# A diffusion-transformer layer on one core: stores issued later in the program, and modulation sums transposed in single banks

## The chip, the cores and the metric

The kernel runs on one core of a Trainium2 chip. The metric is device time in microseconds (us), the median of the runs made. TensorE (PE) multiplies matrices into PSUM, VectorE (DVE), ScalarE (ACT) and GpSimd (POOL) work element by element, and SyncE (SP) issues the DMAs, in the order of its queue. PSUM has eight banks of 128 x 512 fp32 values.

## The reference

One layer of a hybrid diffusion backbone: 1024 latent tokens and 256 context tokens of width 1024. What matters here is the combined input projection, the merge by gates and the modulation:

```python
m_lat = (jax.nn.silu(c) @ w_mod[l] + b_mod[l]).reshape(B_, 1, N_MOD, D)
h_lat = rms_norm(x, norm_mix[l]) * (1.0 + m_lat[:, :, 1]) + m_lat[:, :, 0]
aq, ak, av, bq, bk, bv, cq, cf, cb, ci, cg, gates = features(h_lat, w_in[l], ...)
...
yc = hgrn2_bidir(cq, cf, cb, ci, cg, lbf[l], lbb[l], gn_c[l], s_f, s_b)[0]
ya = window_attn(aq, ak, av, cak, cav, sink_a[l])
yb = global_attn(bq, bk, bv, cbk, cbv)
x_mix = x + m_lat[:, :, 2] * merge_branches(ya, yb, yc, gates, w_branch[l], w_out[l])
h = rms_norm(x_mix, norm_ffn[l]) * (1.0 + m_lat[:, :, 4]) + m_lat[:, :, 3]
x = x_mix + m_lat[:, :, 5] * conv_ffn(h, w_up[l], w_dw[l], b_dw[l], w_down[l])
```

The first two parts of the modulation (`m_lat[0]`, `m_lat[1]`) are needed at the start; the other four, 1024 values each, only from the merge on.

## The kernel before

The layer runs as one program: the first modulation and the norms (to some 60 us), the context's projections, four heads of the recurrence (to some 430 us), the queries, keys and values of the two attentions (`tok_major`, 452 to 680 us), the two attentions (to some 1200 us), merge, output projection, FFN.

**Three matmuls for one.** A weight comes by one DMA as `wr` (L172), ACT casts it to a rounded high part `wh` (L175), DVE makes the low part `wl` (L176). A product is `wh*hh + wh*hl + wl*hh` (L199 to L201 with channels as rows, L209 to L211 with tokens as rows), where `hh` and `hl` are the parts of the normed input. `wr`, `wh` and `wl` have three buffers each.

**The gate unit** (`gate_unit`). Twenty-four of them make the sigmoid gates' inputs. One unit has a weight tile of 128 output channels and two halves of 512 tokens. A half is 24 matmuls into one bank `gz`; then ACT copies it to `gs` (L523, two buffers) and SP stores it to `gate_d` (L524). Outside the attentions both halves lie in one two-bank tile of tag `mm`, and the second half begins when ACT has copied the first. A unit is named by branch and number: `gz27` is branch 2, unit 7, `gs270` and `gs271` its halves.

**The token-major tiles** (`tok_major`, once for each attention `br`). For `u` in 2, 0, 1 (keys and values, then two halves of the queries) eight tiles of 128 tokens: 24 matmuls of 256 columns into `tm`, in a bank of tag `a` for even tiles and `b` for odd ones, two buffers each, taken in turn. `tm117` is attention 1, `u` 1, tile 7. In attention 1, `head_rms` squares on ACT (`hsq`, L1042), sums (L1045) and scales (L1046) on DVE, raises to the power -0.5 on POOL (`hrs`, L1047), and DVE multiplies into `qn` (L610), which is the last read of the bank for queries. Keys have one more, ACT's copy of the values into `qo` (L615). `rope` then makes `t` (L591, two rows) and `qo` (L594, L595), and SP stores `qo` (L616, L618). A gate unit follows each eight tiles.

**The other four parts of the modulation** (`mod_rest`). For each part `j`, eight loads `wmr` (L537, two buffers) are added up on DVE into `macc` (L539, L541); then eight transposes (L546) into an `mm` tile and one reduction along the free axis (L547) give the 1024 values, and `b_mod` is added (L548). `weave` puts one step of it between every few steps of `tok_major`.

**What sets the order.** The code's order decides which buffer a tile gets. The order on each engine is set by the framework's scheduler, which draws an instruction ahead when, by its own estimate, its operands are ready earlier; loads of weights have a raised priority. Each engine then runs its list strictly in that order.

Of the kernel before, what the change touches and what calls it, by code (L numbers as in the profile page):

```python
# [9 lines left out]
F32 = mybir.dt.float32  # L10
# [4 lines left out]
AX = mybir.AxisListType  # L15
# [3 lines left out]
P = 128  # L19
D = 1024  # L20
KT = D // P
# [70 lines left out]
def build(tc, ins, out, dbg=None):  # L92
    nc = tc.nc
    V, A, G, T, SP = nc.vector, nc.scalar, nc.gpsimd, nc.tensor, nc.sync
    with ExitStack() as top:
# [21 lines left out]
        def mm2(name):  # L117
            return ps.tile([P, 2, 512], F32, tag="mm", name=name)
# [160 lines left out]
        with ExitStack() as s0:  # L279
# [214 lines left out]
            for h in range(CH):  # L494
# [6 lines left out]
                for d in range(2):  # L501
# [2 lines left out]
                        T.matmul(u, kt[:, d, c], cV[:, c, h], start=c == 0, stop=c == 1)  # L504
                    A.copy(st_ctx[:, h, d], u)

        def gate_unit(pool, n, i, mode):

            w = w_unit(ins["w_cm"][U_C["gate"] + n * 8 + i], KT, P)
            for hf in range(2):  # L510
                if mode == "b":
                    z = bank("b", f"gz{n}{i}{hf}", (P, 512))
                else:
                    if hf == 0:
                        z2 = mm2(f"gz{n}{i}")
                    z = z2[:, hf]
                for k in range(KT):
                    gemm_cm(z, (w[0][:, k:k + 1], w[1][:, k:k + 1]), H, slice(hf * 512, hf * 512 + 512),
                            k0=k, first=k == 0, last=k == KT - 1)
                    if k < KT - 1:  # L520
                        yield
                gs = pool.tile([P, 512], F32, tag="gs", name=f"gs{n}{i}{hf}", bufs=2)
                A.copy(gs, z)  # L523
                SP.dma_start(gate_d[n, i][:, hf * 512:hf * 512 + 512], gs)  # L524
                yield

        def gate_units(pool, units, mode):
# [3 lines left out]
        def mod_rest(pool):  # L531

            for j in range(4):
                acc = pool.tile([P, D], F32, tag="macc", name=f"macc{j}", bufs=1)
                for k in range(KT):
                    wm = pool.tile([P, D], F32, tag="wmr", name=f"wmr{j}{k}", bufs=2)
                    SP.dma_start(wm, ins["w_mod"][k * P:(k + 1) * P, (j + 2) * D:(j + 3) * D])  # L537
                    if k == 0:
                        V.tensor_scalar(out=acc, in0=wm, scalar1=scc[:, k, 0:1], scalar2=None, op0=ALU.mult)  # L539
                    else:  # L540
                        V.scalar_tensor_tensor(out=acc, in0=wm, scalar=scc[:, k, 0:1], in1=acc,  # L541
                                               op0=ALU.mult, op1=ALU.add)
                    yield
                pm2 = mm2(f"pm2{j}").rearrange("p a (b c) -> p (a b) c", c=P)
                for i in range(KT):
                    T.transpose(pm2[:, i], acc[:, i * P:(i + 1) * P], ident)  # L546
                V.reduce_sum(out=mods[:, j], in_=pm2, axis=AX.X)  # L547
                V.tensor_tensor(out=mods[:, j], in0=mods[:, j], in1=bmod[:, (j + 2) * 8:(j + 3) * 8], op=ALU.add)  # L548
            V.scalar_tensor_tensor(out=af, in0=mods[:, 2], scalar=1.0, in1=gains[:, 1], op0=ALU.add, op1=ALU.mult)
            yield  # L550
# [5 lines left out]
        with ExitStack() as sc:  # L556
            c1 = Aligned(sc.enter_context(tc.tile_pool(name="c1", bufs=1, side="right", reuse_waits="tile")))
            masks = c1.tile([P, NMASK, HB], U32, tag="masks", name="masks")
            SP.dma_start(masks, ins["hmask"])
            late = []  # L560
            for h in range(CH):
                late = hgrn_head(nc, c1, h, proj, early, mm2, bank, ident, masks, lb, oml, st_ctx, gnc, mhalf, y_d, late)
            for n, i in gates[:4]:
                for j, _ in enumerate(gate_unit(c1, n, i, "mm")):
                    if late and j % 8 == 7:
                        late.pop(0)()

        stx.close()


        with ExitStack() as sp3:
            p3 = Aligned(sp3.enter_context(tc.tile_pool(name="p3", bufs=2, side="right", reuse_waits="tile")))
            cs = p3.tile([P, LT, 2, 32], F32, tag="cs", name="cs", bufs=1)
            SP.dma_start(cs, ins["rope"])

            tabs = {}
            for nm, g in (("A", None), ("q", qnb), ("k", knb)):
                tb = p3.tile([P, LT, 2, 2, 32], F32, tag=f"tb{nm}", name=f"tb{nm}", bufs=1)
                for r in range(2):
                    if g is None:  # L580
                        G.tensor_copy(tb[:, :, :, r], cs)
                    else:
                        G.tensor_tensor(out=tb[:, :, :, r], in0=cs,
                                        in1=g[:, None, None, r * 32:(r + 1) * 32].to_broadcast([P, LT, 2, 32]),
                                        op=ALU.mult)
                tabs[nm] = tb

            def rope(src, nh, tt, tab, dst, nm):
                t12 = p3.tile([P, 2, nh, 64], F32, tag="t12", name=f"t12{nm}")
                for w in range(2):  # L590
                    V.tensor_tensor(out=t12[:, w], in0=src,  # L591
                                    in1=tab[:, tt, w].rearrange("p r c -> p (r c)")[:, None, :].to_broadcast([P, nh, 64]),
                                    op=ALU.mult)
                V.tensor_tensor(out=dst[:, :, 0:32], in0=t12[:, 0, :, 0:32], in1=t12[:, 1, :, 32:64], op=ALU.subtract)  # L594
                V.tensor_tensor(out=dst[:, :, 32:64], in0=t12[:, 0, :, 32:64], in1=t12[:, 1, :, 0:32], op=ALU.add)  # L595

            def tok_major(br):
                for u in (2, 0, 1):
                    ws = [w_unit(ins["w_tm"][(br * 3 + u) * 2 + kh], 4, 256) for kh in range(2)]
                    for tt in range(LT):  # L600
                        nm = f"{br}{u}{tt}"
                        z = bank("ab"[tt % 2], f"tm{nm}", (P, 256))
                        gemm_tm(z, ws, H, slice(tt * P, (tt + 1) * P))
                        nh = 4 if u < 2 else 2
                        o = p3.tile([P, 256], F32, tag="qo", name=f"qo{nm}", bufs=3)
                        src = z[:, :nh * 64].rearrange("p (h e) -> p h e", h=nh)
                        if br == 1:
                            rs = head_rms(nc, p3, z[:, :nh * 64], nh, nm, mhalf)
                            qn = p3.tile([P, nh, 64], F32, tag="qn", name=f"qn{nm}")
                            V.tensor_tensor(out=qn, in0=src, in1=rs[:, :, None].to_broadcast([P, nh, 64]), op=ALU.mult)  # L610
                            src = qn
                        tab = tabs["A"] if br == 0 else tabs["q" if u < 2 else "k"]
                        rope(src, nh, tt, tab, o[:, :nh * 64].rearrange("p (h e) -> p h e", h=nh), nm)
                        if u == 2:
                            A.copy(o[:, 128:], z[:, 128:])  # L615
                            SP.dma_start(kv_d[br][2 + tt], o)  # L616
                        else:
                            SP.dma_start(q_d[br][tt][:, u * 256:(u + 1) * 256], o)  # L618
                        yield
                    for _ in gate_unit(p3, *gates[4 + br * 3 + (2, 0, 1).index(u)], "mm"):  # L620
                        yield

            mr = mod_rest(p3)
            weave((tok_major(0), 72), (some(mr, 20), 20))
            weave((tok_major(1), 72), (mr, 13))


        n0 = 10 + GATES_A
        for br, units in ((0, gates[10:n0]), (1, gates[n0:])):
            with ExitStack() as sa:  # L630
                ap_ = Aligned(sa.enter_context(tc.tile_pool(name=f"at{br}", bufs=2, side="right", reuse_waits="tile")))
                nf = 16 * len(units)
                gen = gate_units(ap_, units, "b")
                attention(tc, nc, ap_, br, ins, kv_d[br], q_d[br], y_d, mm2, bank, ident, identr, gen, nf)
                for _ in gen:
                    raise RuntimeError("filler left")
        hpool.close()


# [574 lines left out]
def weave(*gens):  # L1214

    gens = [[g, max(n, 1), 0] for g, n in gens if g is not None]
    while gens:
        gens.sort(key=lambda e: e[2] / e[1])
        e = gens[0]
        try:  # L1220
            next(e[0])
            e[2] += 1
            if e[2] > 4 * e[1]:
                raise RuntimeError("step count")
        except StopIteration:
            gens.remove(e)
# [350 lines left out]
```

## Time and profile before

| | |
|---|---|
| median of 3 runs | 2129.76 us (2128.22 to 2130.08) |
| profiled execution | 2129.82 us, span 2127.9 us |
| busy in the span | PE 2085.8, DVE 1380.5, ACT 1001.2, POOL 288.1 us |
| PE's waits that are longest in sum | for `w_mod` at the start 10.2, for `wl` in `tm` 3.3, for `gs` in `gz` 3.1 us |

Busy time of PE counts matmuls, which overlap; a share of 98% says that PE seldom waits. Where it waits, the lists of waits name the instruction that ended the wait. A wait of another engine costs time only where PE comes to wait for what is behind it.

### The profile page before, as it was taken

The page shows a single profiled execution, that of the slowest core. Times are in us where ns is not written, and L with a number is a line of the kernel's source. Part 1 is how long each engine was busy: PE and PEld are TensorE (multiplying, and loading weights), DVE is VectorE, ACT ScalarE, POOL GpSimd, SP SyncE. Part 2 cuts the span into 40 slices and gives each one's busy share as a digit, 9 for nine tenths or more (in the row PEclk, how much of TensorE's full clock was granted, in tenths as well). Part 3 has the DMA queues.
Part 4 walks back from the last instruction along what each step waited for, and adds up shares of the span by engine and source line. Part 5 has one row for each costly group of instructions (what it writes and reads, how often), then busy time and mean ns, then how long its engine had stood idle before and what let it go on. Part 6 is the DMA issues. An engine that isn't in the chain of part 4 may idle for free.

```text
span 2127.9 us, 30555 instructions
## 1 busy us (share of the span) xinstructions
PE 2085.8 (98%) x11686; PEld 1743.1 (82%) x11686; DVE 1380.5 (65%) x2299; ACT 1001.2 (47%) x1761; POOL 288.1 (14%) x257
## 2 busy tenths in 40 slices
PE   7999999999999999999999999999999999999997
PEld 4888888888988888878888788888888888888887
DVE  4736756636665777678887746569777777664423
ACT  4333333311123777678888734346445544453222
POOL 0000000010021222100000000011333344100111
PEclk9999999999999999999999999999999999999999
DMA  9511111136543211211100354641222222285342
GB/s 359 207 44 36 46 50 41 46 113 214 186 137 123 78 59 41 80 55 35 35 28 28 115 200 142 194 156 55 99 79 89 80 80 88 81 287 201 109 126 86
DMA packets 95490, 229.28 MB, mean 108 GB/s; under 512 B 10736, under 2 KB 35824, under 8 KB 94320
## 3 DMA queue, kind: packets, MB, share of 16 engines
q1 hardware_dynamic: 95344, 227.33, 32.1%
q8 instruction: 92, 1.51, 0.3%
q14 instruction: 54, 0.44, 0.1%
HBM read 181.68 MB, written 45.61 MB: 107 GB/s over the span
## 4 chain that ended last, share of the span: by engine, by line
PE 69%; DVE 3%; ACT 2%; issue 1%; DMA 1%; POOL 1%; SPq 0%; DVEq 0%; ACTq 0%; POOLq 0%
PE pp L1321 4%; PE gz L199 3%; PE dn L929 3%; PE dn L928 3%; PE dn L930 3%; PE gz L200 3%; PE gz L201 3%; PE up L852 2%; PE up L853 2%; PE up L854 2%; PE po L1307 2%; PE po L1308 2%; PE br L200 2%; PE br L201 2%; PE br L199 2%; PE upd L853 2%
## 5 line engine op out<-in xcount | busy, mean ns | idle before, releaser
L175 ACT CAST wh<-wr 128x1024 fp32r<-128x1024 f32 (+1 forms) x139 | 145.1, 1044 | 398.7 <-PE dn L929 69.1
L176 DVE TENSOR_TENSOR wl<-wr,wh 128x1024 fp32r<-128x1024 f32 (+1 forms) x139 | 171.1, 1232 | 221.1 <-ACT wh L175 206.7
L1326 DVE TENSOR_TENSOR pl<-pp,ph 128x512 fp32r<-128x512 f32 x236 | 159.3, 687 | 29.2 <-ACT ph L1325 23.5
L199 PE MATMUL gz<-hh,wh 128*128 128x512 f32 x384 | 156.3, 408 | 3.1 <-ACT gs L523 3.1
L1325 ACT CAST ph<-pp 128x512 fp32r<-128x512 f32 x236 | 135.7, 587 | 37.4 <-PE pp L1321 35.3
L201 PE MATMUL gz<-hh,wl 128*128 128x512 f32 x384 | 152.3, 397 | 0.0
L200 PE MATMUL gz<-hl,wh 128*128 128x512 f32 x384 | 152.1, 396 | 0.0
L210 PE MATMUL tm<-wl,hh 128*128 128x256 f32 x384 | 108.9, 283 | 3.3 <-DVE wl L176 3.3
L209 PE MATMUL tm<-wh,hh 128*128 128x256 f32 x384 | 108.9, 284 | 0.9 <-ACT qo L615 0.9
L211 PE MATMUL tm<-wh,hl 128*128 128x256 f32 x384 | 108.6, 283 | 0.0
L1307 PE MATMUL po<-ph,VHL 128*128 128x512 f32 x236 | 106.1, 450 | 1.4 <-ACT ph L1325 1.0
L929 PE MATMUL dn<-ac,wh 128*128 128x512 f32 x256 | 99.7, 390 | 0.0
L930 PE MATMUL dn<-ac,wl 128*128 128x512 f32 x256 | 99.6, 389 | 0.0
L928 PE MATMUL dn<-ac,wh 128*128 128x512 f32 x256 | 99.6, 390 | 0.0
L1308 PE MATMUL po<-pl,VHL 128*128 128x512 f32 x236 | 97.1, 411 | 0.1
L199 PEld LDWEIGHTS gz<-hh,wh 128*128 128x128 f32 x384 | 72.7, 189 | 17.2 <-ACT gs L523 5.2
L201 PEld LDWEIGHTS gz<-hh,wl 128*128 128x128 f32 x384 | 72.5, 189 | 15.0
L200 PEld LDWEIGHTS gz<-hl,wh 128*128 128x128 f32 x384 | 72.8, 190 | 11.6
L210 PEld LDWEIGHTS tm<-wl,hh 128*128 128x128 f32 x384 | 73.7, 192 | 4.3 <-DVE wl L176 4.0
L1321 PE MATMUL pp<-ident,plat 128*128 128x128 f32 x512 | 76.6, 273 | 0.0
L1321 PEld LDWEIGHTS pp<-ident,plat 128*128 128x128 f32 x512 | 62.7, 140 | 16.9 <-DVE pl L1326 1.2
L199 PE MATMUL br<-yh,wh 128*128 128x512 f32 x192 | 74.3, 390 | 1.6 <-ACT yh L1468 1.6
(1420 smaller groups left out, 5898.7 us busy)
## 6 DMA issues: line engine op xcount, KB each, us to landing
wr<-in_w_cm SPq DMA_DIRECT2D x48, 512.0 KB, 3.7
wr<-in_w_up SPq DMA_DIRECT2D x44, 512.0 KB, 3.5
wr<-in_w_down SPq DMA_DIRECT2D x33, 512.0 KB, 3.5
wmr<-in_w_mod SPq DMA_DIRECT2D x32, 512.0 KB, 4.5
gate_d<-gs SPq DMA_DIRECT2D x48, 256.0 KB, 2.3
sgt<-gate_d SPq DMA_DIRECT2D x24, 512.0 KB, 3.4
act_d<-u SPq DMA_DIRECT2D x22, 512.0 KB, 2.6
st<-act_d SPq DMA_DIRECT2D x44, 256.0 KB, 4.5
```

The costliest lines, as they stand in the source:

```text
L175: A.copy(hi[:, :n], raw[:, :n])
L176: (lo_eng or V).tensor_tensor(out=lo[:, :n], in0=raw[:, :n], in1=hi[:, :n].bitcast(F32), op=ALU.subtract)
L199: T.matmul(psl, wh[:, k, c], hh[:, k0 + k, cols], start=s, stop=False)
L200: T.matmul(psl, wh[:, k, c], hl[:, k0 + k, cols], start=False, stop=False)
L201: T.matmul(psl, wl[:, k, c], hh[:, k0 + k, cols], start=False, stop=e)
L210: T.matmul(psl, hh[:, k, toks], wl[:, k % 4, :], start=False, stop=False)
L928: T.matmul(z, w[0][:, c], h[0], start=s, stop=False)
L929: T.matmul(z, w[0][:, c], h[1], start=False, stop=False)
L930: T.matmul(z, w[1][:, c], h[0], start=False, stop=e)
L1307: T.matmul(po, vv, ph, start=n == 0, stop=False)
L1321: T.transpose(pp[:, h], PT(h, n), ident)
L1326: V.tensor_tensor(out=pl, in0=pp, in1=ph.bitcast(F32), op=ALU.subtract)
```

## The change

It does three things. The stores of `gs` and `qo` are put on a list and issued later in the code: a gate's half in the middle of the next half (after its fifth k step), a `qo` one tile later; the list is emptied at the end of each stage. `qo` has four buffers for three. And each modulation sum is transposed into two single banks of tag `b`, four transposes and one reduction each, in place of one two-bank tile of tag `mm`. (Lines after the change are higher by 7 to 14; the stores all have L512.)

```diff
+        stores = []
+        def later(keep=0):
+            while len(stores) > keep:
+                SP.dma_start(*stores.pop(0))
...
         def gate_unit(pool, n, i, mode):
...
                     if k < KT - 1:
                         yield
+                    if k == 4:
+                        later()
                 gs = pool.tile([P, 512], F32, tag="gs", name=f"gs{n}{i}{hf}", bufs=2)
                 A.copy(gs, z)
-                SP.dma_start(gate_d[n, i][:, hf * 512:hf * 512 + 512], gs)
+                stores.append((gate_d[n, i][:, hf * 512:hf * 512 + 512], gs))
...
-                pm2 = mm2(f"pm2{j}").rearrange("p a (b c) -> p (a b) c", c=P)
-                for i in range(KT):
-                    T.transpose(pm2[:, i], acc[:, i * P:(i + 1) * P], ident)
-                V.reduce_sum(out=mods[:, j], in_=pm2, axis=AX.X)
+                for i2 in range(2):
+                    pm2 = bank("b", f"pm2{j}{i2}")
+                    for i in range(4):
+                        T.transpose(pm2[:, i], acc[:, (4 * i2 + i) * P:(4 * i2 + i + 1) * P], ident)
+                    V.reduce_sum(out=mods[:, j, 4 * i2:4 * i2 + 4], in_=pm2, axis=AX.X)
...
-                        o = p3.tile([P, 256], F32, tag="qo", name=f"qo{nm}", bufs=3)
+                        o = p3.tile([P, 256], F32, tag="qo", name=f"qo{nm}", bufs=4)
...
-                            SP.dma_start(kv_d[br][2 + tt], o)
+                            stores.append((kv_d[br][2 + tt], o))
                         else:
-                            SP.dma_start(q_d[br][tt][:, u * 256:(u + 1) * 256], o)
+                            stores.append((q_d[br][tt][:, u * 256:(u + 1) * 256], o))
+                        later(1)
                         yield
```

`later()` also stands behind each of the first four gate units, behind both calls of `tok_major`, and behind each attention.

**How the order moves: SP's queue at the end of the recurrence.** `gs230` and `gs231` are the halves of the last gate unit there, `wr46` is the weight of the next one, `cs` the table for the rotation, `wmr00` the first load of the modulation, `qo020` the first tile. Before:

```order
L172 DMA wr45_4002<-in_w_tm 128x1024
L524 DMA gate_d_104<-gs230_3591 128x512
L524 DMA gate_d_104<-gs231_3618 128x512
L172 DMA wr46_4282<-in_w_cm 128x1024
L574 DMA cs_3626<-in_rope 128x512
L537 DMA wmr00_3683<-in_w_mod 128x1024
```

After:

```order
L172 DMA wr45_4001<-in_w_tm 128x1024
L512 DMA gate_d_104<-gs230_3591 128x512
L512 DMA gate_d_104<-gs231_3618 128x512
L172 DMA wr46_4283<-in_w_cm 128x1024
L585 DMA cs_3626<-in_rope 128x512
L546 DMA wmr00_3682<-in_w_mod 128x1024
```

Nothing moved here; the stores have a new line. In all of SP's queue four pairs of neighbours change places.

**PE between the halves of the gate unit `gz01`**, where the fourth sum is transposed; the last two transposes follow nine matmuls later, before and after alike. Before:

```order
L199 MATMUL gz01_5894<-hh_336,wh58_5890 128x512
L200 MATMUL gz01_5894<-hl_337,wh58_5890 128x512
L201 MATMUL gz01_5894<-hh_336,wl58_5891 128x512
L546 MATMUL pm23_5934<-ident_89,macc3_5135 128x128 x6
L199 MATMUL gz01_5894<-hh_336,wh58_5890 128x512
```

After:

```order
L199 MATMUL gz01_5899<-hh_336,wh58_5895 128x512
L200 MATMUL gz01_5899<-hl_337,wh58_5895 128x512
L201 MATMUL gz01_5899<-hh_336,wl58_5896 128x512
L556 MATMUL pm230_5939<-ident_89,macc3_5141 128x128 x4
L556 MATMUL pm231_5945<-ident_89,macc3_5141 128x128 x2
L199 MATMUL gz01_5899<-hh_336,wh58_5895 128x512
```

The six transposes stand where they stood, but the last two of them write another bank.

**DVE before the weight `wl56`**, in the middle of `u` 0 of attention 1. Before:

```order
L1046 TENSOR_SCALAR hrs105_5388<-hrs105_5388 128x4
L610 TENSOR_TENSOR qn105_5392<-tm105_5360,hrs105_5388 128x256
L541 SCALAR_TENSOR_TENSOR macc3_5135<-wmr37_5910,scc_83,macc3_5135 128x1024
L591 TENSOR_TENSOR t12105_5394<-qn105_5392,tbq_3631 128x256 x2
L1045 TENSOR_REDUCE hrs106_5428<-hsq106_5426 128x4
L594 TENSOR_TENSOR qo105_5385<-t12105_5394 128x4x32
L595 TENSOR_TENSOR qo105_5385<-t12105_5394 128x4x32
L1046 TENSOR_SCALAR hrs106_5428<-hrs106_5428 128x4
L176 TENSOR_TENSOR wl56_5553<-wr56_5550,wh56_5552 128x1024
L610 TENSOR_TENSOR qn106_5432<-tm106_5400,hrs106_5428 128x256
```

After:

```order
L1060 TENSOR_SCALAR hrs105_5393<-hrs105_5393 128x4
L550 SCALAR_TENSOR_TENSOR macc3_5141<-wmr37_5915,scc_83,macc3_5141 128x1024
L605 TENSOR_TENSOR qo104_5350<-t12104_5359 128x4x32
L606 TENSOR_TENSOR qo104_5350<-t12104_5359 128x4x32
L621 TENSOR_TENSOR qn105_5397<-tm105_5365,hrs105_5393 128x256
L1059 TENSOR_REDUCE hrs106_5433<-hsq106_5431 128x4
L602 TENSOR_TENSOR t12105_5399<-qn105_5397,tbq_3631 128x256 x2
L1060 TENSOR_SCALAR hrs106_5433<-hrs106_5433 128x4
L605 TENSOR_TENSOR qo105_5390<-t12105_5399 128x4x32
L606 TENSOR_TENSOR qo105_5390<-t12105_5399 128x4x32
L621 TENSOR_TENSOR qn106_5437<-tm106_5405,hrs106_5433 128x256
L176 TENSOR_TENSOR wl56_5558<-wr56_5555,wh56_5557 128x1024
```

A step of `macc` now stands between the scaling of `hrs` and `qn`, where POOL's power runs (so in tiles 101, 102, 104 and 105), and `wl56` stands behind `qn106`.

## Rows read from the trace of the kernel before

**Rows 1.** The page, busy us of each engine (share of the span), instructions.

```profile
PE 2085.8 (98%) x11686; PEld 1743.1 (82%) x11686; DVE 1380.5 (65%) x2299; ACT 1001.2 (47%) x1761; POOL 288.1 (14%) x257
```

**Rows 2.** Waits of PE over the span: us in total, times, longest us.

```profile
PE tm L210 <- DVE wl L176: 3.3, 2, 2.0
PE gz L199 <- ACT gs L523: 3.1, 3, 2.2
...
PE tm L209 <- ACT qo L615: 0.9, 1, 0.9
```

**Rows 3.** Stretches: length, busy us by engine, then PE's granted clock, DMA share, GB/s.

```profile
488.10:491.50 3.40, 1.04 (x6) 0.84 (x7) 3.31 (x9) 1.96 (x4) 0.00 (x0) 1.00 0.72 200
...
598.60:602.00 3.40, 3.40 (x10) 2.63 (x9) 0.00 (x0) 0.00 (x0) 0.00 (x0) 0.50 0.62 222
602.00:605.40 3.40, 3.40 (x17) 2.77 (x16) 0.47 (x1) 0.00 (x1) 0.00 (x0) 1.00 0.00 0
```

**Rows 4.** Waits of SP's queue over the span.

```profile
SPq L524 <- ACT gs L523: 163.4, 33, 14.9
```

**Rows 5.** The tile `qo`: what ended its engines' idle time (us, times).

```profile
  DVE t L591: 25.8, 7
  DVE qn L610: 22.3, 8
```

**Rows 6.** The reduction of line 547: duration in ns, first and last start.

```profile
L547 DVE TENSOR_REDUCE mods<-pm x4: 1215/1218/1224, 512.0 to 674.3; 128x8 f32<-128x1024 f32 x4
```

**Rows 7.** Timelines of PE and DVE, sum 0: start, us, engine, line [idle before].

```profile
510.57 1.03 PE L546 MATMUL pm<-ident,macc 128*128 128x128 f32 x8
510.76 0.76 DVE L591 TENSOR_TENSOR t<-tm,tbA 128x256 f32<-128x256 f32 x2 [1.60 <-PE tm L211]
```

**Rows 8.** The same at sum 1.

```profile
555.73 1.03 PE L546 MATMUL pm<-ident,macc 128*128 128x128 f32 x8
...
555.32 0.75 DVE L591 TENSOR_TENSOR t<-tm,tbA 128x256 f32<-128x256 f32 x2
```

**Rows 9.** Timelines of PE and ACT, sum 2.

```profile
594.93 0.82 PE L546 MATMUL pm<-ident,macc 128*128 128x128 f32 x6
597.98 0.50 PE L199 MATMUL gz<-hh,wh 128*128 128x512 f32 x1 [2.23 <-ACT gs L523]
...
597.17 0.27 ACT L615 COPY qo<-tm 128x128 f32<-128x128 f32 x1 [2.59 <-DVE qn L610]
597.34 0.59 ACT L523 COPY gs<-gz 128x512 f32<-128x512 f32 x1
```

**Rows 10.** Timelines of PE, DVE and POOL, sum 3.

```profile
669.48 0.82 PE L546 MATMUL pm<-ident,macc 128*128 128x128 f32 x6
670.32 0.50 PE L199 MATMUL gz<-hh,wh 128*128 128x512 f32 x1
...
672.67 0.42 DVE L610 TENSOR_TENSOR qn<-tm,hrs 128x256 f32<-128x256 f32 x1 [1.19 <-POOL hrs L1047]
...
671.63 1.01 POOL L1047 TENSOR_TENSOR hrs<-hrs,mhalf 128x4 f32<-128x4 f32 x1 [4.60 <-DVE hrs L1046]
```

**Rows 11.** Timeline of DVE before `wl56`, and of PE that waits for it.

```profile
624.75 0.16 DVE L1046 TENSOR_SCALAR hrs<-hrs 128x4 f32<-128x4 f32 x1
...
626.99 0.42 DVE L610 TENSOR_TENSOR qn<-tm,hrs 128x256 f32<-128x256 f32 x1 [0.90 <-POOL hrs L1047]
...
629.93 0.16 DVE L1046 TENSOR_SCALAR hrs<-hrs 128x4 f32<-128x4 f32 x1
631.27 0.42 DVE L610 TENSOR_TENSOR qn<-tm,hrs 128x256 f32<-128x256 f32 x1 [1.19 <-POOL hrs L1047]
...
634.28 1.22 DVE L176 TENSOR_TENSOR wl<-wr,wh 128x1024 fp32r<-128x1024 f32 x1
...
635.56 0.39 PE L210 MATMUL tm<-wl,hh 128*128 128x256 f32 x1 [1.35 <-DVE wl L176]
```

**Rows 12.** Timeline of PE in the first attention.

```profile
779.26 0.55 PE L1321 MATMUL pp<-ident,pw 128*128 128x128 f32 x3 [0.18 <-ACT QT L1288]
```

More of the change, by code (lines that the diff above doesn't have):

```diff
@@ L566, in build @@
                         late.pop(0)()
+            later()
         stx.close()
@@ L625, in build @@
             weave((tok_major(1), 72), (mr, 13))
+            later()
         n0 = 10 + GATES_A
@@ L636, in build @@
                     raise RuntimeError("filler left")
+                later()
         hpool.close()
```

## The prediction

> **What bounds the kernel now.** I read the page's busy times first. TensorE (PE) is busy for 98% of a span of 2127.9 us [rows 1], so an edit of stores and banks can only give back waits of PE or make new ones. All of PE's idle time is 42.1 us, and the stretch that the change touches (the projection of queries and keys, 452 to 680 us) holds four waits of note, read from PE's timeline: 0.86 us at 473, 1.98 and 0.37 us around 490, 2.23 us at 596 and 1.35 us at 634; 6.8 us in all. The list of waits names what ended them: `wl`, the low half of a weight that VectorE (DVE) makes, and `gs`, ScalarE's (ACT) copy of a finished half of a gate tile [rows 2]. The table by stretches adds one thing: in the 3.4 us from 598.6, just behind the 2.23 us wait, PE's granted clock was 0.50, the lower of its two levels (1.2 against 2.4 GHz), and then 1.00 again. Those 3.4 us did 1.7 us of work. The two waits around 490 us, 2.35 us together, left the clock at 1.00 [rows 3].
>
> The queue of DMA issues (SP) waits far more: 163 us in 33 waits for `gs` at the gate stores alone [rows 4]. That counts only where a load stands behind a waiting store and lands too late, so the first question is whether the stores really leave their places.
>
> **The stores.** In the built program they don't. The 48 gate stores and 48 stores of queries, keys and values stand on SP where they stood, before the same weight loads; only their line number is new. Four pairs of neighbours swap in the whole queue, such as one weight load with one load of modulation weights, and none of these is waited for in [rows 2]. What the change says of the stores is therefore worth 0 here. The rope table `cs`, whose lateness holds up the first tiles and the wait at 473 us, still stands behind `gs231` and `wr46`. The fourth `qo` buffer frees ACT's copy and DVE's writes from the landing of a store three tiles back, but ACT's waits before `qo` ended with DVE's `t` and `qn`, never with a DMA [rows 5]: 0 again.
>
> **The transposed sums.** Each of four modulation sums was eight transposes into a two-bank tile of tag `mm` and one DVE reduction. It becomes two times four transposes, each into a bank of tag `b`, and two reductions. PE's work is the same. DVE's row of 1.22 us [rows 6] becomes two rows of half the size: between 0.61 us each (half the row) and 1.22 (the whole row), and I take 0.7, as the size halves and a start is paid twice. DVE is not the bound, so this costs only where something queues behind it. What matters is the tag: `b` has two buffers, taken in turn by every second projection tile, so each half now waits until DVE or ACT has read the tile that held its bank.
>
> *Sum 0, 510 us.* `pm200` needs the bank of `tm001`, `pm201` that of `tm003`; both were read long before. But `tm005` now needs `pm200` reduced. PE reaches the eight transposes at 510.57 [rows 7] and needs 0.8 us; the new order puts six matmuls of `tm006` there (0.72 us), and the reduction follows DVE's `t` row (510.76 + 0.76) and ends near 512.2, against PE's 512.1: **+0.1 us**.
>
> *Sum 1, 556 us.* `pm211` needs `tm017` read. DVE's two `t` rows end at 556.07; PE has begun `pm210` at 555.73 and comes to `pm211` at 556.2 [rows 8]: **0**.
>
> *Sum 2, 595 us.* `pm221` needs ACT's copy `qo127`, which ends at 597.17 + 0.27 = 597.44. PE is there at 595.4 and waits. But it then waits for `gs270`, right behind on ACT, until 597.93, exactly as it does now [rows 9]. The wait is split by two transposes and not made longer: **0**. It is also why the wait doesn't go away with the move out of `mm`: it was never for a bank that the sums held.
>
> *Sum 3, 670 us.* Here is the main term. PE comes to the transposes at 669.48 and runs six of them in 0.84 us with no wait, since the `mm` buffer is free. In the new order four go to `pm230` and the fifth, at about 669.95, to `pm231`, in the bank of `tm117`. That bank is free once DVE's `qn117` has read it, and this row runs from 672.67 to 673.09, behind a GpSimd power that takes until 672.64 [rows 10]. DVE's order there is the old one, so nothing brings it forward, and the chain starts with PE's own last tiles, so it moves with PE. PE waits from 669.95 to about 673.1, runs two transposes and goes on with `gz01` near 673.4, where it was at 670.32: **+3.1 us**. The gate's own wait for `gs010`, over by then, goes under it. Bounds: 2.9 (a start right at the end of the row) and 3.3. Nothing behind it gives time back, as the loads for the attention stand on SP behind `gs011`, which PE's gate tile ends.
>
> **The clock.** The wait of 2.23 us was followed by 3.4 us at half clock, the 1.98 and 0.37 us around 490 by none [rows 3, 9]. The new wait is longer than any of these, so I count one such fall behind it, **+1.7 us**, with 0 as its other end. The fall at 599 us I leave as it is; if the split wait spares it, that is -1.7.
>
> **The order on DVE before `wl56`.** PE's wait at 634 is for `wl56`. It stood before `qn106`, now behind it, and so behind one more GpSimd power. I walked DVE's new order from 604.93 with the old rows: steps of 0.33 (`hrs` sum), 0.34 (`qn`), 0.68 (`t`), 0.40 (`qo`) and 1.19 us (`macc`) from start to start; from the scaling of `hrs` to `qn` 1.34 us with nothing between, as at 629.93, and 2.24 us with a `macc` between, as at 624.75 [rows 11]. The second reduction is 0.55 us shorter than the old one at the start. `qn102` comes at 620.3, `qn104` at 628.45, `qn106` at 635.0, and `wl56` runs from 635.35 to 636.5, where it ended at 635.50. PE's wait grows from 1.35 to 2.4 us: **+1.0 us**. Were the power hidden whole behind `macc` (four places, 0.9 us each), the wait would be gone: -1.35 is the lower end. With one more `macc` of 1.19 in front it is +2.2, the upper end.
>
> The two rows at 624.75 and 626.99 show power and `macc` slowing each other, though not one after the other in full. The Trainium skill, page "SBUF — State Buffer", section "Who interferes with whom", has it that a DVE instruction with two SBUF inputs and a GpSimd one that reads SBUF get a shared port in turn, each for its whole length. By that rule this term would be +2.2 and the sum 2136.4; by the rows it is +1.0, and the sum goes by them.
>
> **The attention.** Three times (once every 35.5 us, as at 779.26) PE waits 0.18 us for `QT` [rows 12]. The new order has the transposes one matmul earlier and the ACT copy ahead of two copies of 0.37 us, so these go: **-0.5 us**. Some ten more neighbours swap in the second attention; its larger waits come before these, and I take 0, give or take 0.5.
>
> **The sum.** The profiled execution took 2129.82 us (span 2127.9 and 1.9 around it), 0.06 over the median, so it stands for it. 2129.82 + 0.1 + 3.1 + 1.7 + 1.0 - 0.5 = **2135.2 us**, 0.26% slower.
>
> **The rivals.**
> - *The clock stays up* behind the new wait: 2133.5, and 2132.5 if `wl56` is no later either. For it: it stayed up after 2.35 us of waits around 490. Against it: 3.1 us is longer and in one piece. It decides whether the change is slower at all, since it ends within 0.2%. Chance 0.25.
> - *A second fall.* The wait for `wl56`, at 2.4 us, is as long as the one that was followed by a fall at 599, and the clock falls there too: 2136.9. It decides from the point where DVE starts `wl56` as late as 635.4. Chance 0.14.
> - *Power and `macc` in turn.* Each power behind a `macc` waits for all of it: 1.19 + 1.34 = 2.53 us from the scaling to `qn` where the row has 2.24, 0.3 more at four places, 1.2 in all: 2136.4. Against it: the one pair of that kind in this stretch [rows 11]. Chance 0.05. The Trainium skill has it as a rule, on the page "SBUF — State Buffer" named above.
> - *The bank of `tm117` is free in time.* If DVE read `tm117` before 669.95, 2.7 us sooner than now, the main term and its fall would go: 2130.4, and 2128.7 if the split wait also spares the old fall. Against it: DVE and GpSimd follow each other there with hardly a gap. With the wait for `wl56` gone as well it would be 2126.4, still within 0.2%. Chance 0.07.
> - *The stores do what the title says.* Then `wr46` and `cs` would be issued ahead of `gs231`, and at most the 0.86 us at 473 and the 2.35 us around 490 would go: 2132.0. Against it: the order of SP. Chance 0.03.
>
> **How the numbers follow.** The forecast has 0.46. A measurement here tells about 0.2%, 4.3 us, from no change: the limits are 2125.5 and 2134.0. Slower: the forecast's 0.46, the second fall's 0.14 and the turns' 0.05, together 0.65. Faster: no case reaches it, and 0.02 stands for what I don't see. Within: the rest, 0.33. The range runs from 2131.8 (no fall, `wl56` no later, 2.9 for the main term, another 0.5 off in the attention) to 2138.1 (the second fall, with +2.2 for `wl56`). The 0.07 of the bank in time lies below it, some 0.06 of the tails beyond either end.
>
> **What would show it.** In the profile after: one wait of PE of some 3 us at a transpose of the fourth sum near 671 us, released by DVE's `qn`; a stretch of 3.4 us at clock 0.50 behind it; PE's wait for `wl` near 635 at 2.4 us; the wait at 596 in two pieces with the same end; SP's gate stores at the same distance from their neighbours. I am wrong if that transpose waits for under 1 us, or if the waits at 473 and 490 us shrink.

## The result and the profile after

The changed kernel takes 2134.39 us against 2128.84 us of the kernel before (medians of 13 runs each), a ratio of 1.0025 with a 95% interval of 1.0017 to 1.0033: slower, and inside the forecast range (2131.8 to 2138.1, forecast 2135.2). The profiled execution has a span of 2132.5 us, 4.6 more than before; it is the median one, while that of before (2129.82 us) lies 1.0 over the median. The page's first part answers [rows 1]; PE's list of waits answers [rows 2]:

```profile
PE 2090.5 (98%) x11686; PEld 1745.9 (82%) x11686; DVE 1382.4 (65%) x2303; ACT 1000.0 (47%) x1761; POOL 291.0 (14%) x257
```

```profile
PE tm L210 <- DVE wl L176: 3.2, 2, 2.0
PE pm L556 <- DVE qn L621: 3.1, 1, 3.1
...
PE pm L556 <- ACT qo L626: 1.8, 1, 1.8
```

Two waits of PE at the transposes (line 556) are new: 3.1 us for `qn`, and 1.8 us for `qo`, which stands where the wait for `gs` stood. PE's busy time is 4.7 us longer for the same number of matmuls, which is the first sign of a slower clock. The table by stretches, which answers [rows 3], says where (length, busy us by engine, PE's granted clock, DMA share, GB/s):

```profile
596.50:599.90 3.40, 3.40 (x9) 2.64 (x8) 0.15 (x1) 0.00 (x0) 0.00 (x0) 0.50 0.66 236
...
671.60:675.00 3.40, 3.17 (x9) 2.60 (x10) 2.03 (x6) 0.00 (x0) 0.00 (x0) 0.50 0.70 242
...
1207.50:1210.90 3.40, 3.40 (x13) 2.93 (x13) 3.21 (x6) 1.52 (x4) 0.00 (x0) 0.50 0.88 324
```

Three stretches in which PE worked ran at half clock, where before had one: the old one near 597, one at the new wait, and one at 1207.

**The fourth sum**, PE and then DVE, against [rows 10]:

```profile
668.15 0.60 PE L556 MATMUL pm<-ident,macc 128*128 128x128 f32 x4
671.83 0.69 PE L556 MATMUL pm<-ident,macc 128*128 128x128 f32 x2 [3.08 <-DVE qn L621]
672.17 0.78 PE L199 MATMUL gz<-hh,wh 128*128 128x512 f32 x1
```

```profile
670.01 0.16 DVE L1060 TENSOR_SCALAR hrs<-hrs 128x4 f32<-128x4 f32 x1
671.35 0.42 DVE L621 TENSOR_TENSOR qn<-tm,hrs 128x256 f32<-128x256 f32 x1 [1.18 <-POOL hrs L1061]
...
673.02 0.68 DVE L557 TENSOR_REDUCE mods<-pm 128x4 f32<-128x512 f32 x1
```

Four transposes go at once; the fifth stands until `qn117` has read its bank (671.35 + 0.42 = 671.77) and starts 0.06 us later. The first matmul behind them takes 0.78 us where it took 0.50: the half clock. The halved reduction takes 0.68 us.

To see where the 4.6 us come from, one can count PE's matmuls from the start and compare the times at which the same number is reached:

| place (time before) | after minus before, us | what lies between |
|---|---|---|
| 474 | -1.2 | the wait at 473 (0.86) is missing |
| 492 | -2.0 | the wait for `wl` near 490: 1.14 for 1.98 |
| 604 | -2.0 | third sum: no change |
| 636 | -1.35 | wait for `wl56`: 2.03 for 1.35 |
| 672 | +3.15 | fourth sum, wait and clock |
| 872 | +4.6 | 0.3 near 701 (the wait for `qs_q`, below), then four steps in the first attention |
| 1209 | +4.1 | |
| the end | +4.6 | |

### The profile page after: what moved, and what is told of

It is laid out like the page before. It is cut to its first block, busy times and chain, and to the rows that moved or that the text cites. A ratio compares the mean times of both kernels' runs of the same rounds, so it can differ in the third digit from the quotient of the medians.

```text
span 2132.5 us, 30547 instructions
## 1 busy us (share of the span) xinstructions
PE 2090.5 (98%) x11686; PEld 1745.9 (82%) x11686; DVE 1382.4 (65%) x2303; ACT 1000.0 (47%) x1761; POOL 291.0 (14%) x257
## 4 chain that ended last, share of the span: by engine, by line
PE 68%; DVE 3%; ACT 2%; issue 1%; POOL 1%; DMA 1%; SPq 0%; DVEq 0%; POOLq 0%; ACTq 0%
PE pp L1335 4%; PE gz L199 3%; PE dn L943 3%; PE dn L942 3%; PE dn L944 3%; PE gz L200 3%; PE gz L201 3%; PE up L866 2%; PE up L867 2%; PE up L868 2%; PE po L1321 2%; PE po L1322 2%; PE br L200 2%; PE br L201 2%; PE br L199 2%; PE upd L867 2%
## 5 line engine op out<-in xcount | busy, mean ns | idle before, releaser
L747 ACT ACTIVATE u<-c,cw 128x1024 f32<-128x1024 f32 x38 | 47.4, 1246 | 62.2 <-DVE c L903 33.2
```

## The experiments

Each is timed side by side with the kernel before on the same chip; a ratio stands with its 95% interval.

**The sums alone** (`e1_sums_only`): the kernel before, with

```diff
-                pm2 = mm2(f"pm2{j}").rearrange("p a (b c) -> p (a b) c", c=P)
...
+                for i2 in range(2):
+                    pm2 = bank("b", f"pm2{j}{i2}")
...
```

> The kernel before with the four sums in single banks and nothing else. Theory (the banks are the cause): PE's wait of 3.1 us at the fourth sum near 671 us and 3.4 us of half clock behind it, the wait for wl56 near 635 at 2.0 us instead of 1.35, and PE's order in the attentions as in the kernel before; so +4.8 and +0.7, in all +5.5 us, ratio 1.0026. Rival (the later stores cost the time): not over +1 us, ratio under 1.0005.

Measured: 1.0020 (1.0011 to 1.0029). The wait at the fourth sum is 3.09 us, and `wl56` is waited for 2.43 us. Here the clock fell behind both (table by stretches):

```profile
634.80:638.20 3.40, 3.40 (x10) 2.62 (x9) 2.47 (x7) 0.00 (x0) 1.85 (x1) 0.50 0.76 252
672.40:675.80 3.40, 2.81 (x8) 2.33 (x9) 2.28 (x6) 0.00 (x0) 0.08 (x1) 0.50 0.67 221
```

So the banks carry most of the loss; the later stores are not needed for it.

**The stores alone** (`e2_stores_only`): the changed kernel, with the sums as before:

```diff
-                for i2 in range(2):
-                    pm2 = bank("b", f"pm2{j}{i2}")
...
+                pm2 = mm2(f"pm2{j}").rearrange("p a (b c) -> p (a b) c", c=P)
...
```

> The changed kernel with the sums back in a two-bank tile: only the stores' place in the code and the fourth qo buffer are new. In SP's queue one pair of neighbours differs from before; on PE the transposes of the next query stand one matmul earlier, four times in the first attention. Theory: nothing changes up to 680 us, and each of the four places costs 0.23 us, as in the profile of after, where PE goes from matmuls to transposes and back once more: +0.9 us, ratio 1.0004. The prediction had this term at -0.5 us, ratio 0.9998. Rival (the stores cost the time): +3 us or more, ratio 1.0015 or more, with waits at gate tiles.

Measured: 1.0006 (0.9997 to 1.0014), so a loss of 3 us or more is out; +0.9 us fits and 0 is not excluded by the times. The trace shows the places. PE's timeline near 800 us in the kernel before, and the same place here:

```profile
799.37 0.39 PE L1307 MATMUL po<-ph,VHL 128*128 128x512 f32 x1
799.60 0.39 PE L1308 MATMUL po<-pl,VHL 128*128 128x512 f32 x1
799.83 0.46 PE L1286 MATMUL pq<-identr,qs_q 128*128 128x128 f32 x4
800.12 0.35 PE L1387 MATMUL sa<-KH,QT 128*128 128x256 f32 x1
800.32 0.28 PE L1388 MATMUL sa<-KL,QT 128*128 128x256 f32 x1
```

```profile
797.13 0.50 PE L1320 MATMUL po<-ph,VHL 128*128 128x512 f32 x1
797.47 0.46 PE L1299 MATMUL pq<-identr,qs_q 128*128 128x128 f32 x4
797.86 0.50 PE L1321 MATMUL po<-pl,VHL 128*128 128x512 f32 x1
798.19 0.28 PE L1400 MATMUL sa<-KH,QT 128*128 128x256 f32 x1
798.31 0.28 PE L1401 MATMUL sa<-KL,QT 128*128 128x256 f32 x1
```

From `po<-ph` to the second `sa` it is 0.95 us before (799.37 to 800.32) and 1.18 here (797.13 to 798.31), 0.23 more with no wait in it: transposes between two products of 512 columns cost more than behind them. There are three such places (near 766, 801 and 837 us in the kernel before); at a fourth, near 872, a product of 512 columns now stands among the next tile's `sa`, and 0.5 us go. By the count of matmuls this kernel loses 1.3 us over the four, and the changed kernel 1.3 as well.

One wait is longer too: PE waits 1.55 us near 698 for `qs_q`, the first attention's queries, where the kernel before waits 0.51. It follows the landing of their load `qf_q`, 4.9 us after its issue here and 3.9 before. Over the twelve kernels the latest such landing was 3.0 to 4.9 us, and the wait went with it, from none to 1.55. With the stores later it was 3.7 to 4.9 us, with the stores in place 3.0 to 4.6. These overlap, and no run here settles whether the later stores lengthen it.

**The fourth sum alone, and all but the fourth.** `e4_sum3_only` is the kernel before with the new form for one sum, `e3_sum3_in_mm` the changed kernel with the old form for that sum (the condition is `j < 3` there):

```diff
+                if j == 3:
+                    for i2 in range(2):
+                        pm2 = bank("b", f"pm2{j}{i2}")
...
+                else:
+                    pm2 = mm2(f"pm2{j}").rearrange("p a (b c) -> p (a b) c", c=P)
...
```

> The kernel before with the fourth sum alone in single banks; order on all engines as before but for that sum. Theory: a wait of 3.1 us at 671 us and a clock fall of 1.7 us behind it, all else as before: +4.8 us, ratio 1.0022. Rival (the clock fall belongs to something else in the change, or PE gives the wait back later): +3.1 us, ratio 1.0015, or less, with the clock at 1.00 behind the wait.

> The changed kernel with the fourth sum alone back in a two-bank tile; order on all engines as in the changed kernel but for that sum. Theory: the wait of 3.1 us at 671 and the clock fall behind it go, the rest stays: +1.6 us against before, ratio 1.0008, about 4.8 us less than the changed kernel. Rival (the wait is only shifted to the gate's second half or to the next weight): about as slow as the changed kernel, ratio 1.002 or more.

Measured: 1.0023 (1.0014 to 1.0032) for the fourth sum alone and 1.0007 (0.9998 to 1.0016) for all but it. One sum makes the whole difference that the times can tell. In its trace, PE's timeline and the table by stretches:

```profile
668.83 0.69 PE L548 MATMUL pm<-ident,macc 128*128 128x128 f32 x2 [3.11 <-DVE qn L617]
```

```profile
668.70:672.10 3.40, 3.27 (x9) 2.70 (x10) 1.93 (x6) 0.00 (x0) 0.00 (x0) 0.50 0.76 243
672.10:675.50 3.40, 3.40 (x17) 2.76 (x17) 0.86 (x2) 0.00 (x0) 0.00 (x0) 1.00 0.04 14
```

The same 3.4 us hold 9 matmuls and then 17: the fall costs half of what PE works in it, 1.6 us. In the kernel with all but the fourth, PE is busy for 11.98 of the 12 us from 668, at full clock; its wait for `wl56` is 2.61 us, and no fall follows it. The traced execution of the fourth sum alone was the fastest of its eleven (2129.20 us, median 2132.68), so its trace shows the wait and the fall, but not what the others spent beside them.

**Another bank** (`e5_sums_in_a`): the changed kernel, with

```diff
-                    pm2 = bank("b", f"pm2{j}{i2}")
+                    pm2 = bank("a", f"pm2{j}{i2}")
```

> The changed kernel with the single banks of the sums under tag a, the tag of the even tiles, in place of b; order on DVE, ACT, POOL and SP word for word as in the changed kernel, on PE five matmuls of tile 6 stand elsewhere at the first sum. Theory (the wait is for the last reader of one bank): the bank is now that of tm116, read some 5 us earlier than that of tm117, so the wait of 3.1 us and its clock fall go, and +1.6 us against before stay (0.7 for wl56, 0.9 in the attention), ratio 1.0008. Rival (single banks and split reductions cost by themselves): as slow as the changed kernel, ratio 1.002 or more.

Measured: 1.0005 (0.9997 to 1.0014). PE's timeline has the six transposes of the fourth sum in one go again:

```profile
666.54 0.82 PE L556 MATMUL pm<-ident,macc 128*128 128x128 f32 x6
667.38 0.50 PE L199 MATMUL gz<-hh,wh 128*128 128x512 f32 x1
```

With DVE, ACT, POOL and SP in the same order and the same eight reductions, another tag takes the loss away. What cost was neither the single bank nor the split reduction, but which tile had last used the bank. (PE's order differs as well, at the first sum, where neither kernel waits.)

**A longer chain** (`e11_sum3_long`): the fourth sum alone, with two more powers ahead of the one that `qn117` waits for:

```diff
+    if nm == "117":
+        for k in range(2):
+            s = pool.tile([P, 4], F32, tag="hrx", name=f"hrx{k}", bufs=1)
+            nc.gpsimd.tensor_tensor(out=s, in0=r, in1=mhalf[:, :nh], op=ALU.pow)
     nc.gpsimd.tensor_tensor(out=r, in0=r, in1=mhalf[:, :nh], op=ALU.pow)
```

> The kernel before with the fourth sum alone in single banks, as in an earlier run (+4.8 us expected, ratio 1.0023 measured), and two more powers of 1.0 us on GpSimd, into a scratch tile, ahead of the power that qn of tm117 waits for; all other order is the same. Theory (PE's wait follows the chain to the bank's last reader one for one, and the clock fall behind it costs its 1.7 us once, however long the wait): wait 5.1 us, one stretch of 3.4 us at half clock, +6.8 us against before, ratio 1.0032. Rivals: the fall grows with the wait (two stretches, +8.5 us, ratio 1.0040), or the wait does not follow the power since another read of the bank is the last (+4.8 us, ratio 1.0023).

Measured: 1.0032 (1.0019 to 1.0044). The timeline and the table by stretches:

```profile
674.33 0.69 PE L548 MATMUL pm<-ident,macc 128*128 128x128 f32 x2 [5.24 <-DVE qn L617]
```

```profile
669.08:672.80 3.72, 0.00 (x1) 0.00 (x0) 1.42 (x3) 0.19 (x1) 2.02 (x2) 1.00 0.66 192
672.80:679.60 6.80, 5.27 (x15) 4.20 (x16) 2.56 (x7) 0.00 (x0) 1.01 (x1) 0.50 0.29 108
```

The wait follows the chain one for one: with the two powers, 2.09 us, 3.11 becomes 5.24. The half clock, though, was not one stretch of 3.4 us but 6.8. Of these 1.5 lie in the wait itself, where the clock costs nothing, and 5.27 in work, which costs 2.6 us where the shorter wait paid 1.6. My expectation that the fall costs the same however long the wait is fell here; the rival's two full stretches of work did not come either. The ratio cannot tell the two apart.

**The gate's halves in tiles of their own.** The wait for `gs` near 596 led to four more kernels: the second half of a gate unit waits for the copy of the first only since both share one tile. In effect (by one more mode of `gate_unit`) they change that:

```diff
-                    if hf == 0:
-                        z2 = mm2(f"gz{n}{i}")
-                    z = z2[:, hf]
+                    z = mm2(f"gz{n}{i}{hf}")[:, 0]
```

(`e6_halves`, `e8_halves_a_only` and `e9_halves_only` do so for the six gate units among the projection tiles, `e10_halves_all` also for four at the end of the recurrence. `e6_halves` starts from the changed kernel, the others from the kernel before, `e8_halves_a_only` with the sums in tag `a`.)

> The changed kernel, but each half of a gate unit among the projection tiles takes an mm tile of its own (of which it uses one bank), so the second half need not wait until ACT has copied the first. The order then has both halves one behind the other and the fourth sum 9 gate matmuls later, 2.1 us. Theory: the bank of tm117 is still waited for, but only for 3.1 - 2.1 = 1.0 us and without a clock fall; the waits for gs near 490 and 595 us go (0.4 and 1.8 us, and the clock fall behind the second); against before about -2.5 + 1.0 + 0.7 + 0.9 = 0.1 us, ratio 1.000 (0.999 to 1.001). Rival (the wait at 595 is DVE's and POOL's chain, and the gate copies are not what counts): another wait of about 2 us turns up at the next tile or weight, ratio 1.002 or more.

> The kernel before (stores where they were) with two edits: a tile of its own for each half of a gate unit among the projection tiles, and the sums in single banks of tag a. Theory: no wait at any sum, none for gs near 490 and 595, no clock fall from 590 to 680, the attention as before: -2.5 us, and -4.2 with the fall that before had at 599, ratio 0.998 to 0.999. Rival (a later wait takes it back, at a weight low half or at the attention's first transposes): ratio 1.000.

> The kernel before with the one edit that each half of a gate unit among the projection tiles takes an mm tile of its own; the sums stay in two-bank mm tiles. Theory: as the kernel with sums in tag a, since the sums find the mm tile of the first half free by then: -2.5 to -4.2 us, ratio 0.998 to 0.999. Rival (the sums need an mm tile while both hold gate halves, so single banks for the sums are what makes such an edit possible): a new wait of 1 us or more for gs at the second and fourth sum, ratio 1.000 or more.

> The kernel of the run before last (a tile of its own for each gate half among the projection tiles, sums in two-bank tiles; ratio 0.9953) with the same edit for the four gate units at the end of the recurrence. Theory: PE had no wait for gs there, so nothing is to be had from the waits: the same time within 1 us, ratio 0.995. Rival (the halves one behind the other let the gate's loads and the next weights run ahead, as they did from 480 us on): another 1 us or more, ratio 0.9945 or less.

Measured: 0.9970 (0.9958 to 0.9982) for the changed kernel with it; 0.9956 (0.9944 to 0.9968) and 0.9953 (0.9941 to 0.9965) for the kernel before with it, with sums in `a` and in two-bank tiles; 0.9956 (0.9944 to 0.9969) with ten units. In the first of these the sum stands 9 gate matmuls later and the wait shrinks nearly as worked out, 1.25 for 1.0 us; all four transposes of the second bank wait, and the clock stays at 1.00 (timeline of PE, then the table by stretches):

```profile
662.94 0.66 PE L558 MATMUL pm<-ident,macc 128*128 128x128 f32 x4 [1.25 <-DVE qn L623]
```

```profile
655.00:680.00 25.00, 23.60 (x117) 19.31 (x116) 11.62 (x28) 7.62 (x18) 2.01 (x2) 1.00 0.52 157
```

Its ratio lies below the 0.999 to 1.001 that I had expected, and the gain of `e8_halves_a_only` and `e9_halves_only` is 2 to 4 times what I had expected; `e10_halves_all` came out as expected, no faster than `e9_halves_only`. The table by stretches of the kernel before with that one edit (`e9_halves_only`) shows PE busy without a break at the places of all four waits near 490, 596 and 634:

```profile
480.00:500.00 20.00, 20.00 (x126) 18.11 (x125) 13.91 (x26) 4.72 (x8) 0.00 (x0) 1.00 0.82 258
590.00:610.00 20.00, 20.00 (x140) 18.65 (x139) 14.76 (x34) 5.77 (x11) 3.56 (x3) 1.00 0.61 205
630.00:640.00 10.00, 10.00 (x76) 9.61 (x75) 7.89 (x22) 2.30 (x4) 2.89 (x3) 1.00 0.70 226
```

I had counted the waits for `gs` and the clock behind one of them (0.4 + 2.2 + 1.7). But the order also changes: while the second half had to wait, the scheduler put the next tile's first six matmuls between the halves, and these then waited for that tile's weight. With the halves one behind the other the tile starts a gate half later, and the waits for `wl` (2.0 + 1.35) go as well. That makes 7.6; at 701 us this kernel is 9.7 us ahead in its trace. The count of matmuls assigns most of the rest: around each of the four waits PE loses 0.2 to 0.3 us more than the idle time in the row (2.9 us at the two near 490, whose rows have 1.99 and 0.37), 1.0 in all, and 0.6 is the wait for `qs_q` near 701, which this execution doesn't have (its load landed after 3.0 us). Some 0.5 lies in small steps at the sums, whose eight transposes stand in one go here. It is the kernel to take for its one small edit, 2118.98 us and 0.47% under the kernel before beside it (by the two ratios, 0.7% under the changed one); the times can't tell it from the two at 0.9956. The sums need no single banks for it.

## Why the prediction was right

**The stores: right that they don't move, wrong that this makes them worth 0.** On SP the later stores change one pair of neighbours (a load of queries and a store of the attention's output, in `e2_stores_only`), and they bring no new wait at a gate tile. But the later place in the code did change the order of PE, ACT and DVE in the first attention, which I had not traced back to the stores. The prediction booked these swaps separately, and with the wrong sign.

**The waits at 473 and 490 us: smaller, and not by the change.** I had written that I am wrong if they shrink. They did, by 1.7 us. The DMA rows of before and of after, each from 455 to 492 us (last column: us from issue to landing):

```profile
cs<-in_rope SPq DMA_DIRECT2D x1, 256.0 KB, 5.9
```

```profile
cs<-in_rope SPq DMA_DIRECT2D x1, 256.0 KB, 4.0
```

The rope table came 1.9 us sooner, at the same place in the queue. In the ten other kernels it took 4.6 to 6.0 us; wherever it took 5.1 or less there was no wait of over 0.25 us at 473, and from 5.3 on one of 0.4 to 0.9 us, whether the stores were moved or not. I take that for chance from one execution to the next; no kernel was traced twice.

**Sums 0, 1 and 2: right.** PE has no wait above 0.12 us at the first two. At the third, PE and then ACT, against [rows 9]:

```profile
593.10 0.60 PE L556 MATMUL pm<-ident,macc 128*128 128x128 f32 x4
595.48 0.44 PE L556 MATMUL pm<-ident,macc 128*128 128x128 f32 x2 [1.78 <-ACT qo L626]
595.96 0.50 PE L199 MATMUL gz<-hh,wh 128*128 128x512 f32 x1
...
595.16 0.27 ACT L626 COPY qo<-tm 128x128 f32<-128x128 f32 x1 [2.59 <-DVE qn L621]
```

The second half starts at 595.96, exactly the 2.0 us earlier that PE was early anyway.

**Sum 3: right.** 3.08 for 3.1 us, with the releaser and the place as worked out; 3.09 and 3.11 in two more kernels.

**The clock: right.** At the new wait it fell in the traces of all four kernels that have it, at a price of 1.4 to 1.6 us (and 2.6 behind the longest) for the 1.7 forecast. The rival of a second fall, behind the wait for `wl56`, did not come in the changed kernel's trace, but did in that of the sums alone, where this wait was 2.43 us. The mean granted clock of all timed runs (three decimals each) agrees in kind: 0.9967 for the sums alone and 0.9962 for the fourth sum alone, against 0.9974 for the kernel before beside them, which is 1.4 and 2.6 us of lost clock in 2130 us; 0.9973 and 0.9976 for the two kernels without the wait.

**`wl56`: the size came out, the mechanism did not.** DVE's rows against [rows 11], then PE's:

```profile
623.67 0.16 DVE L1060 TENSOR_SCALAR hrs<-hrs 128x4 f32<-128x4 f32 x1
623.74 1.28 DVE L550 SCALAR_TENSOR_TENSOR macc<-wmr,scc,macc 128x1024 f32<-128x1024 f32 x1
...
625.91 0.42 DVE L621 TENSOR_TENSOR qn<-tm,hrs 128x256 f32<-128x256 f32 x1 [0.49 <-POOL hrs L1061]
...
627.25 0.16 DVE L1060 TENSOR_SCALAR hrs<-hrs 128x4 f32<-128x4 f32 x1
...
628.72 0.28 DVE L606 TENSOR_TENSOR qo<-t 128x128 f32<-128x128 f32 x1
629.90 0.42 DVE L621 TENSOR_TENSOR qn<-tm,hrs 128x256 f32<-128x256 f32 x1 [0.90 <-POOL hrs L1061]
...
632.93 1.22 DVE L176 TENSOR_TENSOR wl<-wr,wh 128x1024 fp32r<-128x1024 f32 x1
...
634.20 0.39 PE L210 MATMUL tm<-wl,hh 128*128 128x256 f32 x1 [2.03 <-DVE wl L176]
```

From the scaling to `qn`, with a `macc` between, it is 2.24 us at 623.67, the price taken from the row of before, but 2.65 us at 627.25. In the four kernels with the new order it is 2.25 at tiles 101 and 102; at 104 it is 2.24 in the changed kernel and 2.65 in the three others, and at 105 it is 2.65 in all four. Neither my 2.24 everywhere nor the 2.53 of the rival in which power and `macc` go in turn fits. But it was the rival's price that was wrong, more than its mechanism. POOL's rows of the same execution: with a `macc` (623.74 to 625.02), with a `macc` and behind it two writes of `qo` (627.32 to 629.00), and with neither:

```profile
623.97 1.91 POOL L1061 TENSOR_TENSOR hrs<-hrs,mhalf 128x4 f32<-128x4 f32 x1 [1.68 <-DVE hrs L1060]
627.56 2.31 POOL L1061 TENSOR_TENSOR hrs<-hrs,mhalf 128x4 f32<-128x4 f32 x1 [1.68 <-DVE hrs L1060]
631.55 1.01 POOL L1061 TENSOR_TENSOR hrs<-hrs,mhalf 128x4 f32<-128x4 f32 x1 [1.68 <-DVE hrs L1060]
```

The first power begins 0.23 us after the `macc` and ends 0.9 after its end, nearly the power's own length of 1.0; the second ends 0.9 after the end of the second `qo`. So the power does seem to stand until these DVE instructions are done, and loses what is left of them. The rule of the Trainium skill (page "SBUF — State Buffer", section "Who interferes with whom") agrees with these rows. In the rival I had charged the whole `macc`, and nothing for the `qo`.

The wait for `wl56` was 1.35, 1.70, 1.37 and 1.37 us in the four kernels with DVE's old order and 2.03, 2.43, 2.61 and 2.44 in the four with the new one: +0.9 in the mean, against the +1.0 forecast. The changed kernel's 0.4 less is its one place less at 2.65. That the term came out nearly right with one or two prices 0.4 too low is in part luck: the rest of my walk was too long. In the changed kernel, with PE 2.0 us early, `qn102`, `qn104` and `qn106` came 0.2, 0.5 and 0.4 us ahead of the times that the walk gave.

**The attention: wrong.** I had the transposes one matmul earlier and took that for the three waits of 0.18 us for `QT`. They are at other transposes: the wait stands in the trace of after as in [rows 12],

```profile
782.87 0.55 PE L1335 MATMUL pp<-ident,pw 128*128 128x128 f32 x3 [0.18 <-ACT QT L1302]
```

and what moved stands near 766, 801, 837 and 872 us, where PE waited for nothing and loses by the move. The term is +1.3, not -0.5. The failed step was to match a swap in the order to a wait in the trace by its distance of 35.5 us alone, without looking which query it was.

**The sum.** With the terms as measured it would be 3.1 + 1.6 + 0.9 + 1.3 = 6.9 us, against a ratio that stands for 3.6 to 7.0. The forecast's 5.4 is nearer to the middle of that interval; with one term 1.8 too low, some of that is luck. The same terms give 5.4 us for the sums alone (the fall at 1.4), 1.3 for the stores alone, 4.7 for the fourth sum alone, 2.2 for all but it and 2.2 for tag `a`; the ratios stand for 4.3, 1.3, 4.9, 1.5 and 1.1, and each sum lies within its interval. The clock adds to the scatter. The old fall at 599 is in three traces (before, after and the longer chain, where the wait ahead of it is 1.78 to 2.23 us) and missing in the five others that keep that wait, at 0.93 to 1.64 us. One near 1207 turns up in three (after, the stores alone, the longer chain) and one at 907 in `e6_halves`; that of after cost little, since before waited 1.55 us for `yh` there and after did not.

## What to carry to other kernels

The bank of a tile is free when its last reader is done, not when its matmuls are: before moving a small job into another tag, look up which tile used that bank last, who reads it, and when. A bank of the neighbouring tag, one tile older, cost nothing here. And where two halves share one tile, the second waits for the copy of the first: tiles of their own, from the same pool, were worth more than anything that was done around them.

## What the runs showed of the hardware

A wait of PE does not tell by its length alone whether the clock falls. Twelve executions were traced, one of each kernel. It fell at all four waits of 3.1 us and over. It also fell behind waits of 2.23 (before and the longer chain, at 596), 2.43 (sums alone, at 632), 2.09 (`e6_halves`, at 905) and 1.78 us (after, at 594), and stayed at 1.00 behind 2.61 (all but the fourth sum, at 632), 2.44 (sums in tag `a`, at 630) and 2.03 us (after, at 632). Near 1207 it fell in three traces where the longest wait of PE just before was 0.97 us. The stretches at half clock were 3.4 us, and 6.8 at the wait of 5.2. In these traces the fall can be counted at a wait as long as the fourth sum's; behind one of 1.8 to 2.6 us it came or not.

Four transposes of 128 columns between two products of 512 columns cost 0.23 us more than the same four behind both (0.95 and 1.18 us by the rows of the two kernels above).

A GpSimd power of 1.0 us took 1.6 to 1.9 us beside one `macc` of 1.28 us, and 2.3 where two writes of `qo` followed the `macc` at once (7 of 8 such places in four kernels).
